# Hybrid streaming encoder: score products on all 128 rows, a plain first up unit, and convolution taps that alternate between channel halves

## The chip, the cores and the metric

The kernel runs on one core of one Trainium2 chip. The metric is the device time of one execution in microseconds (us). A core has a matrix engine (TensorE, PE in the profile, with PEld for its weight loads), a vector engine (VectorE, DVE), an activation engine (ScalarE, ACT), a general engine (GpSimd, POOL), and a sync engine (SyncE, SP) that here issues nearly all transfers. Each takes its own instructions in order and waits on semaphores for the others.

## What is computed

One layer of an encoder for 1024 prompt frames and 64 sample frames (T = 1088), model width 1024. A normed input goes through one projection into four mixers of width 256: a gated depthwise convolution of 31 taps, a "forgetting" attention (fox), a gated recurrence (hgrn), and a "stick-breaking" attention (sb). Then come an output projection, attention to 256 memory frames, and a feed-forward part. Cut to what matters:

```python
s = einsum('bqhd,bkhd->bhqk', q, k) * HEAD_DIM ** -0.5        # fox and sb: 4 heads of 64 each, 1024 x 1024, causal
fox: p = softmax(s + cq - ck);   sb: a = exp(log_sigmoid(z) + sum of log_sigmoid(-z) over later keys)
conv: y = depthwise_conv(a * sigmoid(g), 31 taps) + bias; layer norm over 256 channels; silu
x = x + mix @ w_out;  x = x + mem_attend(rmsnorm(x));  h = rmsnorm(x)
x = x + square(relu(h @ w_up)) @ w_down                       # 1024 -> 4096 -> 1024
```

The sample frames do the same with 512 cached keys ahead of their own.

## The kernel before

**Precision.** A product of two float32 operands is made of high and low parts (`split`, lines 168 to 171: ACT writes the high part, DVE the difference), and three matmuls: high by high, high by low, low by high (`mm3`). `mm` (line 71) issues every matmul.

**Order.** The kernel is written as lanes (projections, attention, convolution, recurrence), Python generators that a loop steps by a virtual clock. Each instruction gets a priority (`tc.cur_priority`, lower first), and a planner lays the instructions of each engine in one fixed order by priority and readiness. Projection matmuls have the lowest rank in the mixer stage (`PR_MM`), so they fill what the lanes leave of PE.

**Attention.** `project_qkv` makes queries, keys and values of a pair of heads (128 rows: head 0 on rows 0 to 63, head 1 on rows 64 to 127). Its sinks write `qT` (two buffers), `kT` (one) and `vn`, chunk by chunk (CH: 512, 256, 320 columns). There are four such pairs in turn: sb0, sb1, fox0, fox1, and `attend` (lines 527 to 597) runs for each. It splits the keys into `kh` and `kl`. For each block of 128 query rows (i = 0 to 7) with n = 128 (i + 1) keys it splits the query columns, makes the scores z of both heads, runs the softmax or stick-breaking chain on ACT and DVE, transposes the result (`key_T`) and multiplies by the values. A score product takes the 64 rows of its head, in three passes. Up to 512 keys both heads' products are issued together, pass by pass; over 512 keys there is one PSUM tile for both heads and they are made one after the other. After the eight blocks comes the sample block: a block-diagonal query tile `qbd` on 128 rows against 512 cached keys (`caches`) and 64 new ones.

**Convolution.** `lane_conv` takes three chunks (352, 352, and 320 prompt columns with 30 + 64 more, 414) and in each the two channel halves: load, gate, then 31 taps, the first a `tensor_scalar` and 30 `scalar_tensor_tensor` (line 773) that add into the same y.

**Feed-forward, up part.** Sixteen units of two column blocks of `w_up` each. A unit uses a Strassen-Winograd scheme: seven half products for eight, over sums of the four quarters of the normed activations (T1 to T4) and of the weights (S1 to S4). Group 0 of the columns (512) is normed early. Group 1 (576) is completed by `dense_add(1, w_mo, ...)`, which calls `forms(m)` after each of its eight row blocks: it adds to the sum of squares, and from m = 4 on it norms two blocks and builds B22, T1, T2, T3 and T4 on DVE and ACT. Everything after it is moved back by `tc.cur_priority += 1200`. Unit 0 then runs like the others, and computes the scale q of group 1 on its way. Unit 0 and unit 1 take B21 and B22 early. Weight tiles `wr`, `wh` and `wl` have two buffers each; the pool `ap` has 16.

Of the kernel before, what the change touches and what calls it, by code (L numbers as in the profile page):

```python
# [8 lines left out]
F32 = mybir.dt.float32  # L9
# [43 lines left out]
def kernel(ctx: ExitStack, tc: tile.TileContext, *args):  # L53
# [155 lines left out]
    hid_d = dram.tile([DFF // P, P, T], F32, name="hid_d")  # L209
    rms_d = dram.tile([P, 576], F32, name="rms_d")  # L210
# [31 lines left out]
    with ExitStack() as pa:  # L242
# [180 lines left out]
    def project_qkv(kind, hp, cq, ck, cv, cache_k, cache_v, outs):  # L423

        cs = slice(hp * P, (hp + 1) * P)
        qT = att.tile([P, T], F32, name="qT", tag="qT")
# [29 lines left out]
        tiles[kind, hp] = qT, kT, vn  # L456
# [70 lines left out]
    def attend(hp, kind, mask, chain, cache_k, cache_v, mix_slot):  # L527
        qT, kT, vn = tiles[kind, hp]
# [3 lines left out]
        hd = [slice(0, 64), slice(64, 128)]  # L532
        fox = kind == "fox"
        for i in range(8):
            n = P * (i + 1)

            zs, aTs = [None, None], []
            q = [wk.tile([P, P], F32R, name=nm, tag=nm, bufs=1) for nm in ("qh", "ql")]
            split(*q, qT[:, i * P:(i + 1) * P])

            def scores(heads):
                for h2 in heads:
                    zs[h2] = score_tile(n, h2)
                for c in range(0, n, 512):
                    w = min(512, n - c)
                    for t, (a, b) in enumerate(((0, 0), (1, 0), (0, 1))):
                        for h2 in heads:
                            mm(zs[h2][:, c:c + w], q[a][hd[h2]], k[b][hd[h2], c:c + w], t == 0,
                               t == 2 and c + w < n and not fox)
# [22 lines left out]
        n = PAST + SS  # L572

        for sl in hd:
            split(qbd[sl, 0, sl], qbd[sl, 1, sl], qT[sl, SP:T])
# [21 lines left out]
        yield 2  # L597
# [126 lines left out]
    CE = 320 + HW + SS  # L724

    def ct_(name, tag, n=CE):
        return hc.tile([P, n], F32, name=name, tag=tag)
# [14 lines left out]
    def lane_conv():  # L742
        tails = [None, None]
        for t0, np_ in ((0, 352), (352, 352), (704, 320)):
# [3 lines left out]
            for ct in range(2):  # L748
                yield Need(ct)
                yield Need(2 + ct)  # L750
                ext = ct_(f"ext{ct}", f"ce{ct}", CE + HW)
# [5 lines left out]
                if last:  # L757
                    V.tensor_copy(out=ext[:, HW + np_:CE - SS + HW], in_=hT[:, ct])
                    nc.sync.dma_start(out=ext[:, CE - SS + HW:], in_=pj_d[ct][:, SP:T])
# [4 lines left out]
                if last:  # L764
                    V.tensor_tensor(out=ext[:, CE - SS + HW:], in0=ext[:, CE - SS + HW:], in1=sg[:, np_:nt], op=ALU.mult)
# [3 lines left out]
                y = ct_(f"y{ct}", f"cy{ct}")  # L769
                V.tensor_scalar(out=y[:, :n], in0=ext[:, 0:n], scalar1=cwT[:, ct, 0:1], scalar2=cvec[:, 0, ct:ct + 1],  # L770
                                op0=ALU.mult, op1=ALU.add)
                for j in range(1, CW):
                    V.scalar_tensor_tensor(out=y[:, :n], in0=ext[:, j:j + n], scalar=cwT[:, ct, j:j + 1], in1=y[:, :n],  # L773
                                           op0=ALU.mult, op1=ALU.add)
                    if j % 3 == 2:
                        yield 0.15 + n / 300.0
                ys.append(y[:, :n])
                exts.append(ext)
            if last:
# [8 lines left out]
            sqs = [ct_(f"sq{ct}", f"ce{ct}", CE + HW) for ct in range(2)]  # L788
            for p0, pn in ((0, n // 2), (n // 2, n - n // 2)):
# [18 lines left out]
                for ct in range(2):  # L808
# [4 lines left out]
                    else:  # L813
                        nc.sync.dma_start(out=mix_d[ct][:, t0 + p0:SP], in_=ys[ct][:, p0:np_])
                        nc.sync.dma_start(out=mix_d[ct][:, SP:T], in_=ys[ct][:, CE - SS:])
# [207 lines left out]
    stage = [att.tile([P, 2 * n], F32, name="mix", tag=tag, bufs=b) for tag, b in (("qT", 2), ("kT", 1), ("vn", 2))]  # L1023
    stage = [t[:, i * n:(i + 1) * n] for t in stage for i in range(2)]
# [244 lines left out]
    for f in (T3, T4):  # L1269
        hb[f] = [[unit("xt" if k else "ap", F32R) for _ in range(2)] for k in range(4)]  # L1270

    sums2 = []

    def forms(m):
# [5 lines left out]
        if m < 4:  # L1280
            return
        k = m - 4
        (h11, h12), (h21, h22) = ((xw[0][i], xw[1][i]) for i in (k, k + 4))
        for i in (k, k + 4):
            normed(1, i, g_ffn, rm1, 0, N2, xw[1][i])
# [4 lines left out]
        split(*hb[B22][k], h22)  # L1290
# [36 lines left out]
    for i in range(NU):  # L1327
# [3 lines left out]
        split(*pa, r1)  # L1331
        s1 = fz.tile([P, 4, P], F32, name="s1", tag="s1", bufs=1)
# [11 lines left out]
        if i < 2:  # L1344
# [6 lines left out]
        plus(halves(c12), halves(c12 if i < 2 else t1), Z[:, :, :HN])  # L1351
        mul2(X, S1, hb[T1], True)
        plus(halves(c22), halves(t1), X[:, :, :HN])
        if i < 2:
# [5 lines left out]
        if i == 0:  # L1360
            q = rms_stats(1, psm, "w", s2=sums2[0])
            rms = unit("tm")
            nc.sync.dma_start(out=rms, in_=rms_d)
            V.tensor_tensor(out=q, in0=q, in1=rms, op=ALU.mult)
# [3 lines left out]
        if i >= 2:  # L1368
# [8 lines left out]
        for m, g, t in ((0, 0, c11), (0, 1, c12), (1, 0, c21), (1, 1, c22)):  # L1377
            t0, n, _ = GR[g]
            nc.sync.dma_start(out=hid_d[2 * i + m][:, t0:t0 + n], in_=t[:, :n])
# [125 lines left out]
```

## Time and profile before

| | us |
|---|---|
| median of 3 runs (1791.69 to 1795.78) | 1795.35 |
| the profiled execution, its own time | 1796.39 |
| its span, first to last instruction | 1794.7 |
| PE busy in the span | 1721.9 |
| DVE busy | 1179.9 |
| ACT busy | 793.2 |
| POOL busy | 103.2 |

The mean granted TensorE clock is 0.987 of full. A busy PE counts the pipeline's length of each matmul (some 0.28 us for a short one), so the step between starts, not the length, is what a matmul costs in a stream.

### The profile page before, as it was taken

What the parts mean: (1) busy time and instruction counts of PE and PEld (TensorE: products, weight loads), DVE (VectorE), ACT (ScalarE), POOL (GpSimd) and SP (SyncE); (2) the same over time, 40 slices, a digit from 0 to 9 for tenths busy, and PEclk for the clock granted to TensorE, in tenths of its full rate; (3) what the DMA queues carried; (4) which work ended last, traced back from release to release, by engine and by line L of the source; (5) the groups of instructions that cost most, each with busy time, mean ns of one, the idle gap of its engine ahead of it and who ended that gap; (6) DMA issues with size and microseconds to landing.
All of it is one profiled execution on the core that took longest, in us unless ns stands there. A gap on an engine that the chain in (4) does not pass through costs nothing.

```text
span 1794.7 us, 29493 instructions
## 1 busy us (share of the span) xinstructions
PE 1721.9 (96%) x11463; PEld 1511.7 (84%) x11475; DVE 1179.9 (66%) x2242; ACT 793.2 (44%) x1615; POOL 103.2 (6%) x201
## 2 busy tenths in 40 slices
PE   7999999999999999999999959999999999999997
PEld 5877757887877788988899949999999999999987
DVE  6455779888979886667777796555556544444435
ACT  6464566456356764346456343433344221222213
POOL 3011202000320210000000000000000000000000
PEclk9999999999999999999999989999999999999999
DMA  8221212222232448232522413333234823332112
GB/s 251 78 78 37 65 47 76 70 68 80 64 116 89 141 139 279 87 95 65 159 77 72 123 49 106 104 116 106 98 97 168 294 90 97 98 97 67 42 35 100
DMA packets 227307, 184.86 MB, mean 103 GB/s; under 512 B 16478, under 2 KB 196127, under 8 KB 227167
## 3 DMA queue, kind: packets, MB, share of 16 engines
q1 hardware_dynamic: 226911, 182.96, 32.7%
q8 instruction: 90, 1.47, 0.3%
q14 instruction: 50, 0.41, 0.1%
q0 software_dynamic: 256, 0.01, 0.0%
HBM read 132.45 MB, written 50.44 MB: 102 GB/s over the span
## 4 chain that ended last, share of the span: by engine, by line
PE 57%; DVE 5%; DMA 2%; ACT 1%; issue 1%; POOL 0%; SPq 0%; DVEq 0%; ACTq 0%; POOLq 0%
PE pz L71 23%; PE pw L71 16%; PE pa L71 8%; PE pq L71 5%; PE pmo L71 1%; PE pms L71 1%; DMA kr<-mkT_d 1%; PE pm L71 1%; DVE wl L171 1%; DVE ap L171 0%; PE pmt L1160 0%; PE pz L1430 0%; DVE tm L1075 0%; ACT wh L74 0%; DMA mix_d<-ho 0%
## 5 line engine op out<-in xcount | busy, mean ns | idle before, releaser
L74 ACT ACTIVATE wh<-wr 128x1024 fp32r<-128x1024 f32 (+1 forms) x180 | 161.4, 905 | 436.5 <-PE pz L71 196.3
L171 DVE TENSOR_TENSOR wl<-wr,wh 128x1024 fp32r<-128x1024 f32 (+1 forms) x180 | 184.6, 1032 | 70.8 <-ACT wh L74 69.8
L71 PE MATMUL pw<-ap,wh 128*128 128x512 f32 x704 | 219.7, 393 | 1.3 <-ACT t L74 0.7
L71 PE MATMUL pz<-ap,wh 128*128 128x288 f32 x960 | 192.5, 294 | 0.4 <-DVE ap L1325 0.4
L71 PE MATMUL pa<-ap,wh 128*128 128x256 f32 (+2 forms) x768 | 187.6, 332 | 2.6 <-DVE xt L1099 2.2
L71 PE MATMUL pm<-hx,wh 128*128 128x512 f32 (+1 forms) x640 | 176.3, 363 | 1.1 <-DVE hx L283 0.8
L71 PE MATMUL pm<-ap,wh 128*128 128x256 f32 (+1 forms) x768 | 164.2, 307 | 0.6 <-ACT vn L74 0.6
L71 PEld LDWEIGHTS pz<-ap,wh 128*128 128x128 f32 x960 | 156.7, 188 | 5.3 <-DVE ap L1325 0.8
L71 PEld LDWEIGHTS pw<-ap,wh 128*128 128x128 f32 x704 | 127.8, 189 | 23.7 <-ACT t L74 1.1
L71 PEld LDWEIGHTS pa<-ap,wh 128*128 128x128 f32 x768 | 132.9, 192 | 13.5 <-DVE xt L1099 2.4
L71 PE MATMUL pw<-ap,wl 128*128 128x512 f32 x352 | 138.1, 392 | 5.6 <-DVE wl L171 5.6
L71 PE MATMUL pz<-ap,wl 128*128 128x288 f32 x480 | 141.0, 294 | 0.0
L71 PEld LDWEIGHTS pm<-ap,wh 128*128 128x128 f32 x768 | 123.5, 191 | 5.4 <-issue 2.1
L71 PE MATMUL pa<-ap,wl 128*128 128x512 f32 (+2 forms) x384 | 127.2, 332 | 0.0
L71 PEld LDWEIGHTS pm<-hx,wh 128*128 128x128 f32 x640 | 110.2, 191 | 19.7 <-issue 1.9
L1325 DVE TENSOR_TENSOR xt<-xt,pz 128x576 f32<-128x576 f32 x56 | 42.2, 753 | 115.5 <-PE pz L71 111.0
L71 PE MATMUL pm<-ap,wl 128*128 128x256 f32 (+1 forms) x384 | 114.1, 297 | 0.0
L71 PE MATMUL pm<-hx,wl 128*128 128x512 f32 (+1 forms) x320 | 112.3, 351 | 0.0
L773 DVE SCALAR_TENSOR_TENSOR y<-ext,cwT,y 128x352 f32<-128x352 f32 (+1 forms) x180 | 106.4, 607 | 1.6
L1325 DVE TENSOR_TENSOR xt<-xt,pw 128x512 f32<-128x512 f32 (+2 forms) x80 | 51.0, 638 | 69.8 <-PE pw L71 67.7
L71 PE MATMUL pq<-ap,wh 128*128 128x512 f32 (+2 forms) x384 | 93.0, 331 | 0.0
L74 ACT ACTIVATE sba<-sba 128x127 f32<-128x127 f32 (+8 forms) x102 | 68.1, 682 | 52.8 <-DVE sba L490 52.0
(376 smaller groups left out, 3645.1 us busy)
## 6 DMA issues: line engine op xcount, KB each, us to landing
wr<-in_w_up_dram SPq DMA_DIRECT2D x32, 512.0 KB
wr<-in_w_down_dram SPq DMA_DIRECT2D x32, 512.0 KB
wr<-in_w_in_dram SPq DMA_DIRECT2D x24, 512.0 KB
hid_d<-ap SPq DMA_DIRECT2D x32, 288.0 KB
aq<-hid_d SPq DMA_DIRECT2D x32, 288.0 KB
wr<-in_w_out_dram SPq DMA_DIRECT2D x16, 512.0 KB
wr<-in_w_mq_dram SPq DMA_DIRECT2D x16, 512.0 KB
wr<-in_w_mo_dram SPq DMA_DIRECT2D x32, 256.0 KB
```

Of the source, the lines that this page charges most:

```text
L71: nc.tensor.matmul(out, lhsT=lhsT, rhs=rhs, start=start, stop=stop, **kw)
L74: nc.scalar.activation(out=out, in_=in_, func=func, **kw)
L171: V.tensor_tensor(out=lo, in0=src, in1=hi.bitcast(F32), op=ALU.subtract)
L773: V.scalar_tensor_tensor(out=y[:, :n], in0=ext[:, j:j + n], scalar=cwT[:, ct, j:j + 1], in1=y[:, :n], op0=ALU.mult, op1=ALU.add)
L1325: eng.tensor_tensor(out=out, in0=a, in1=b, op=ALU.add)
```

## The change

1. **Scores.** The query sink no longer fills `qT`: it writes a staging tile `st` and stores it to DRAM (`q_d`). `attend` loads it back as `q2`, each head's 64 rows twice, on rows 0 to 63 and 64 to 127 (four loads; one buffer). The keys are split as before, and three chained transfers per chunk swap halves so that `k[0]` holds head 0's high part over its low part and `k[1]` head 1's. A score product then runs on 128 rows in two passes (query high, query low), one head after the other; the low by low part comes along. The sample block moves ahead of the eight prompt blocks. The ninth tile of x at the start takes `kT`'s buffer instead of one of `qT`'s.
2. **Convolution.** Chunks of 376, 376 and 272 + 30 + 64 = 366 columns; the taps of the two halves alternate.
3. **First up unit.** Unit 0 uses plain products with the weights as they are (eight half products), of B11, B21, `b12` (new) and B22. After each row block of the last projection `second(m)` norms and splits that block only; `forms(k)` (T1 to T4) runs ahead of unit 1, with priority moved back by 800. The scale q is made between unit 0's two halves.

```diff
+    q_d = dram.tile([4, P, T], F32, name="q_d")
+    k_d = dram.tile([4, HD, SP], F32, name="k_d")
...
-            xt.append((att.tile([P, T], F32, name=f"xt{i}", tag=("vn", "qT")[i - 7])[:, :D] if i >= 7 else
+            xt.append((att.tile([P, T], F32, name=f"xt{i}", tag=("vn", "kT")[i - 7], bufs=(2, 1)[i - 7])[:, :D] if i >= 7 else
...
-        qT = att.tile([P, T], F32, name="qT", tag="qT")
+        slot = len(tiles)
...
-            V.scalar_tensor_tensor(out=qT[:, t0:t0 + n], in0=ps, scalar=HD ** -0.5, in1=rb[:, t0:t0 + n],
+            s = wk.tile([P, 512], F32, name="qT", tag="st")
+            V.scalar_tensor_tensor(out=s[:, :n], in0=ps, scalar=HD ** -0.5, in1=rb[:, t0:t0 + n],
                                    op0=ALU.mult, op1=ALU.mult)
+            nc.sync.dma_start(out=q_d[slot][:, t0:t0 + n], in_=s[:, :n])
...
+        q2 = att.tile([P, 2, T], F32, name="q2", tag="q2", bufs=1)
+        for h2 in range(2):
+            for sl in hd:
+                nc.sync.dma_start(out=q2[sl, h2], in_=q_d[slot][hd[h2]])
         k = [att.tile([P, T], F32R, name=nm, tag=nm, bufs=1) for nm in ("kh", "kl")]
         for t0, n in CH:
             split(*(t[:, t0:t0 + n] for t in k), kT[:, t0:t0 + n])
...
+            kh, kl = (t.bitcast(F32) for t in k)
+            nc.sync.dma_start(out=k_d[slot][:, cols], in_=kh[64:, cols])
+            nc.sync.dma_start(out=kh[64:, cols], in_=kl[:64, cols])
+            nc.sync.dma_start(out=kl[:64, cols], in_=k_d[slot][:, cols])
...
+            q = [wk.tile([P, 2, P], F32R, name=nm, tag=nm, bufs=1) for nm in ("qh", "ql")]
+            split(*q, q2[:, :, i * P:(i + 1) * P])
...
-                    for t, (a, b) in enumerate(((0, 0), (1, 0), (0, 1))):
-                        for h2 in heads:
-                            mm(zs[h2][:, c:c + w], q[a][hd[h2]], k[b][hd[h2], c:c + w], t == 0,
-                               t == 2 and c + w < n and not fox)
+                for h2 in heads:
+                    for c in range(0, n, 512):
+                        w = min(512, n - c)
+                        for t in range(2):
+                            mm(zs[h2][:, c:c + w], q[t][:, h2], k[h2][:, c:c + w], t == 0,
+                               t == 1 and c + w < n and not fox)
...
-        for t0, np_ in ((0, 352), (352, 352), (704, 320)):
+        for t0, np_ in ((0, CN), (CN, CN), (2 * CN, SP - 2 * CN)):
...
+            for j in range(CW):
+                for ct, (y, ext) in enumerate(zip(ys, exts)):
+                    if j == 0:
+                        V.tensor_scalar(out=y, in0=ext[:, 0:n], scalar1=cwT[:, ct, 0:1], scalar2=cvec[:, 0, ct:ct + 1],
+                                        op0=ALU.mult, op1=ALU.add)
+                    else:
+                        V.scalar_tensor_tensor(out=y, in0=ext[:, j:j + n], scalar=cwT[:, ct, j:j + 1], in1=y,
+                                               op0=ALU.mult, op1=ALU.add)
...
+    b12 = [pair(1) for k in range(4)]
...
-    def forms(m):
+    def second(m):
...
+        normed(1, m, g_ffn, rm1, 0, N2, xw[1][m])
+        split(*(hb[B22][m - 4] if m >= 4 else b12[m]), xw[1][m])
+
+    def forms(k):
...
-    dense_add(1, w_mo, HALF * P, KD - HALF, om[HALF:], ps1, store=True, after=forms)
+    dense_add(1, w_mo, HALF * P, KD - HALF, om[HALF:], ps1, store=True, after=second)
...
-    tc.cur_priority += 1200
...
+    ws = [load_w(w_up, 0, KD, m * P) for m in range(2)]
+    tiles = [unit("ap") for _ in range(4)]
+    for m in range(2):
+        W = bank()
+        mul(W, ws[m], hb[B11] + hb[B21], True, slice(0, N1))
+        square(tiles[2 * m][:, :N1], W)
+    q, rms = rms_stats(1, psm, "w", s2=sums2[0]), unit("tm")
+    nc.sync.dma_start(out=rms, in_=rms_d)
+    V.tensor_tensor(out=q, in0=q, in1=rms, op=ALU.mult)
+    for m in range(2):
+        Z = banks()
+        mul2(Z, ws[m], b12 + hb[B22], True)
+        square(halves(tiles[2 * m + 1]), Z[:, :, :HN], halves(q))
+    store_hidden(0, tiles)
+
+    for i in range(1, NU):
...
+        if i == 1:
+            tc.cur_priority += 800
+            for k in range(4):
+                forms(k)
```

## Rows read from the trace of the kernel before

**Rows 1.** Busy time of each engine by stretch (us from the span's start, length, then busy us and instructions of PE, PEld, DVE, ACT, POOL, the granted clock, the DMA share and GB/s).

```profile
60.00:200.00 140.00, 136.69 (x959) 111.39 (x958) 79.77 (x132) 78.09 (x155) 12.55 (x33) 0.98 0.22 63
200.00:500.00 300.00, 289.05 (x2095) 227.35 (x2098) 255.46 (x544) 164.62 (x371) 41.10 (x64) 0.99 0.23 67
500.00:650.00 150.00, 140.00 (x1124) 114.42 (x1130) 132.01 (x291) 98.62 (x240) 30.16 (x34) 1.00 0.38 114
1027.00:1077.00 50.00, 30.96 (x180) 26.40 (x179) 47.65 (x78) 24.07 (x42) 0.00 (x0) 0.83 0.24 71
```

**Rows 2.** PE's timeline from the end of the last projection into unit 0 (start us, us, engine, line, operation, tiles, shapes, count; in brackets the idle time before and what ended it).

```profile
1033.03 0.28 PE L71 MATMUL pa<-ap,wl 128*128 128x256 f32 x1
...
1045.29 1.44 PE L71 MATMUL pr<-tm,ones 128*128 128x320 f32 x2 [10.67 <-DVE tm L1054]
1052.36 0.80 PE L71 MATMUL pw<-ap,wl 128*128 128x512 f32 x1 [5.64 <-DVE wl L171]
...
1061.94 0.53 PE L71 MATMUL pz<-fz,wh 128*128 128x288 f32 x2 [0.34 <-ACT wh L74]
```

**Rows 3.** The chain that ended last, in order of time, over units 2 and 3 (start us, us, what, count).

```profile
1120.96 2.78 PE pw L71 x12
1123.73 6.36 PE pz L71 x48
1130.09 2.74 PE pw L71 x12
...
1142.10 2.78 PE pw L71 x12
```

**Rows 4.** The same chain at the end of the mixer stage, and below it the longest wait of the SP queue from 100 to 660 us (us in total, times, longest us).

```profile
612.28 2.32 DMA hq<-pj_d
...
665.30 4.53 DMA wr<-in_w_out_dram
...
672.21 7.80 PE pa L71 x26
...
SPq L416 <- DVE sp L415: 83.9, 19, 13.3
```

**Rows 5.** PE's timeline at a score block over 512 keys, behind four transposes (sb1, 768 keys).

```profile
266.62 0.60 PE L513 MATMUL pt<-ident,sba 128*128 128x128 f32 x4
267.15 0.50 PE L71 MATMUL z<-kh,qh 64*128 64x512 f32 x1
267.50 0.39 PE L71 MATMUL z<-kh,ql 64*128 64x512 f32 x1
267.73 0.39 PE L71 MATMUL z<-kl,qh 64*128 64x512 f32 x1
...
268.07 0.28 PE L71 MATMUL z<-kh,ql 64*128 64x256 f32 x1
268.19 0.28 PE L71 MATMUL z<-kl,qh 64*128 64x256 f32 x1
268.40 0.23 PE L71 MATMUL z<-mask_s,ident_bf 128*128 128x128 bf16 x1
```

**Rows 6.** PE's timeline at a score block of 128 keys (sb0, both heads in each row).

```profile
63.15 0.28 PE L71 MATMUL z<-kh,ql 64*128 64x128 f32 x2
63.27 0.28 PE L71 MATMUL z<-kl,qh 64*128 64x128 f32 x2
```

**Rows 7.** The view of tile z: one of its three groups of prompt score matmuls (count, ns min/median/max, first and last start, forms).

```profile
L71 PE MATMUL z<-kh,qh x96: 218/436/502, 63.0 to 610.1; 64*128 64x512 f32 x48, 64*128 64x128 f32 x16, 64*128 64x256 f32 x16, 64*128 64x384 f32 x16
```

**Rows 8.** DVE's timeline: three taps of one half in a row, and six that take the halves in turn.

```profile
418.43 1.83 DVE L773 SCALAR_TENSOR_TENSOR y<-ext,cwT,y 128x352 f32<-128x352 f32 x3
...
426.70 3.06 DVE L773 SCALAR_TENSOR_TENSOR y<-ext,cwT,y 128x352 f32<-128x352 f32 x6
```

**Rows 9.** Views of the tiles qT, kT and mix_d (low parts on DVE, and the stores of the four sample blocks); then timelines: the first scores of sb1 on PE, the store of fox0's sample block on SP, the first and third query chunk of fox1 on DVE.

```profile
L171 DVE TENSOR_TENSOR ql<-qT,qh x32: 268/284/537, 62.7 to 600.3; 128x128 fp32r<-128x128 f32 x32
...
L171 DVE TENSOR_TENSOR kl<-kT,kh x12: 419/484/692, 36.7 to 513.1; 128x512 fp32r<-128x512 f32 x4, 128x256 fp32r<-128x256 f32 x4, 128x320 fp32r<-128x320 f32 x4
...
L596 SPq DMA_DIRECT2D mix_d<-os x4: 320/326/338, 197.3 to 643.5; - x4
...
212.60 0.33 PE L71 MATMUL z<-kh,qh 64*128 64x128 f32 x2
...
480.94 0.32 SPq L596 DMA_DIRECT2D mix_d<-os  x1
...
535.76 0.67 DVE L432 SCALAR_TENSOR_TENSOR qT<-pm,rb 128x512 f32<-128x512 f32 x1
...
553.57 0.49 DVE L432 SCALAR_TENSOR_TENSOR qT<-pm,rb 128x320 f32<-128x320 f32 x1
```

**Rows 10.** Timelines at the start: the first write of kT on DVE and the last transposes of x on PE.

```profile
34.46 0.68 DVE L437 TENSOR_TENSOR kT<-pm,rb 128x512 f32<-128x512 f32 x1
...
41.32 0.58 PE L280 MATMUL px<-ident,xt 128*128 128x128 f32 x3
```

**Rows 11.** Busy time by stretch, as in the first group, for the gap ahead of the units.

```profile
1034.00:1064.00 30.00, 11.92 (x43) 8.17 (x44) 29.43 (x46) 15.37 (x27) 0.00 (x0) 0.72 0.04 13
```

**Rows 12.** Groups of DVE instructions from 1034 to 1064 us by shape (count | busy us, mean ns | idle before).

```profile
L171 DVE TENSOR_TENSOR fz<-xt,fz 128x576 fp32r<-128x576 f32 x5 | 3.8, 751 | 0.0
...
L171 DVE TENSOR_TENSOR wl<-wr,wh 128x1024 fp32r<-128x1024 f32 x1 | 1.2, 1218 | 0.0
```

More of the change, by code (lines that the diff above doesn't have):

```diff
@@ L455, in project_qkv @@
         flush()
-        tiles[kind, hp] = qT, kT, vn
+        tiles[kind, hp] = slot, kT, vn
         done.add((kind, hp))
@@ L572, in attend @@
+            n = min(n, SP - t0)
+            cols = slice(t0, t0 + n)
+            kh, kl = (t.bitcast(F32) for t in k)
+            nc.sync.dma_start(out=k_d[slot][:, cols], in_=kh[64:, cols])
+            nc.sync.dma_start(out=kh[64:, cols], in_=kl[:64, cols])
+            nc.sync.dma_start(out=kl[:64, cols], in_=k_d[slot][:, cols])
         n = PAST + SS
-        for sl in hd:
-            split(qbd[sl, 0, sl], qbd[sl, 1, sl], qT[sl, SP:T])
+        for h2, sl in enumerate(hd):
+            split(qbd[sl, 0, sl], qbd[sl, 1, sl], q2[sl, h2, SP:T])
@@ L597, in attend, with scores @@
         yield 2
+        for i in range(8):
+            n = P * (i + 1)
+            zs, aTs = [None, None], []
+            q = [wk.tile([P, 2, P], F32R, name=nm, tag=nm, bufs=1) for nm in ("qh", "ql")]
+            split(*q, q2[:, :, i * P:(i + 1) * P])
+            def scores(heads):
+                for h2 in heads:
+                    zs[h2] = score_tile(n, h2)
+                for h2 in heads:
+                    for c in range(0, n, 512):
[3 more added lines that the diff above has]
+                               t == 1 and c + w < n and not fox)
+                for h2 in heads:
+                    if fox:
+                        for c in range(0, n, 512):
+                            w = min(512, n - c)
+                            mm(zs[h2][:, c:c + w], neg1[:, 2 * hp + h2], ckx[:, c:c + w], False, c + w < n)
+                    mm(zs[h2][:, n - P:n], ident_bf, mask[0], False, True)
+            if n <= 512:
+                scores((0, 1))
+            for h2 in range(2):
+                if n > 512:
+                    scores((h2,))
+                p = chain(zs[h2][:, :n], n)
+                aTs.append(key_T(p, n))
+                yield 0.3 + n / 256.0
+            pv = ps_tr.tile([P, P], F32, name="pv", tag="tr")
+            for j in range(i + 1):
+                for h2 in range(2):
+                    mm(pv[hd[h2]], vn[:, j, hd[h2]], aTs[h2][:, j], j == 0, j == i)
+            o = wk.tile([P, P], F32, name="o", tag="o")
+            evac(o, pv)
+            nc.sync.dma_start(out=mix_d[mix_slot][:, i * P:(i + 1) * P], in_=o)
     prev = [None]
@@ L768, in lane_conv @@
                     V.tensor_copy(out=tails[ct], in_=ext[:, n:n + HW])
[L769 to L777, printed above, removed]
-                exts.append(ext)
+                ys.append(ct_(f"y{ct}", f"cy{ct}")[:, :n])
+                exts.append(ext)
+            for j in range(CW):
[6 more added lines that the diff above has]
+                                               op0=ALU.mult, op1=ALU.add)
+                if j % 3 == 2:
+                    yield 0.3 + n / 150.0
             if last:
@@ L787, in lane_conv @@
             rs = ct_("rs", "c0").rearrange("p (j n) -> p j n", j=2)
-            sqs = [ct_(f"sq{ct}", f"ce{ct}", CE + HW) for ct in range(2)]
+            sqs = [ct_(f"sq{ct}", f"ce{ct}", CN + HW) for ct in range(2)]
             for p0, pn in ((0, n // 2), (n // 2, n - n // 2)):
@@ L1022 @@
     n = GR[0][1]
-    stage = [att.tile([P, 2 * n], F32, name="mix", tag=tag, bufs=b) for tag, b in (("qT", 2), ("kT", 1), ("vn", 2))]
-    stage = [t[:, i * n:(i + 1) * n] for t in stage for i in range(2)]
+    stage = [att.tile([P, 2 * n], F32, name="mix", tag=tag, bufs=b) for tag, b in (("kT", 1), ("vn", 2))]
+    stage.append(att.tile([P, 4 * n], F32, name="mix", tag="q2", bufs=1))
+    stage = [t[:, i * n:(i + 1) * n] for t in stage for i in range(t.shape[1] // n)]
     stage += [wk.tile([P, n], F32, name="mix", tag="st") for _ in range(2)]
@@ L1295, in forms @@
         split(hb[T4][k][0][:, :N1], hb[T4][k][1][:, :N1], h21[:, :N1])
-    dense_add(1, w_mo, HALF * P, KD - HALF, om[HALF:], ps1, store=True, after=forms)
+    dense_add(1, w_mo, HALF * P, KD - HALF, om[HALF:], ps1, store=True, after=second)
     pm1.close()
     psm = ctx.enter_context(tc.tile_pool(name="psm", bufs=2, space=PSUM))
-    tc.cur_priority += 1200
+    for f in (T3, T4):
+        hb[f] = [[unit("xt" if k else "ap", F32R) for _ in range(2)] for k in range(4)]
     for t in t1s:
@@ L1325, in plus, with store_hidden @@
         eng.tensor_tensor(out=out, in0=a, in1=b, op=ALU.add)
-    for i in range(NU):
+    def store_hidden(i, tiles):
+        for m, g, t in zip((0, 0, 1, 1), (0, 1, 0, 1), tiles):
+            t0, n, _ = GR[g]
+            nc.sync.dma_start(out=hid_d[2 * i + m][:, t0:t0 + n], in_=t[:, :n])
+    ws = [load_w(w_up, 0, KD, m * P) for m in range(2)]
[13 more added lines that the diff above has]
+    for i in range(1, NU):
         r1 = fetch_w(w_up, 0, KD, 2 * i * P)
@@ L1359 @@
         square(c11[:, :N1], W)
[L1360 to L1364, printed above, removed]
         mul2(Z, S3, hb[T3], False)
@@ L1367 @@
         square(c22, c22, q)
-        if i >= 2:
+        if i > 1:
             mul2(X, S4, hb[B22], False)
@@ L1376 @@
         square(c21[:, :N1], c21[:, :N1])
-        for m, g, t in ((0, 0, c11), (0, 1, c12), (1, 0, c21), (1, 1, c22)):
-            t0, n, _ = GR[g]
-            nc.sync.dma_start(out=hid_d[2 * i + m][:, t0:t0 + n], in_=t[:, :n])
+        store_hidden(i, (c11, c12, c21, c22))
     fz_ctx.close()
```

66 lines of the change are left out of this document (14 added, 52 removed).

## The prediction

> **What bounds the kernel now.** First the busy times by stage [rows 1]. From 60 to 650 us, the mixer stage, TensorE (PE) is busy 566 of 590 us, VectorE (DVE) 85% from 200 to 500 and 88% from 500 to 650. From 1027 to 1077 us it is the reverse: PE 30.96 of 50 us, DVE 47.65. So two places are on the path that sets the end: a PE-bound mixer stage with DVE close behind, and a gap at the head of the feed-forward stage where PE waits for DVE. I read the gap in PE's timeline [rows 2]: the last matmul of the projection before it starts at 1033.03, then PE idles 10.67 and 5.64 us behind DVE, and full-rate products begin at 1061.94. Behind it the chain of waits is PE alone, in steady units: from one unit's first pw at 1120.96 to the next at 1142.10 is 21.1 us [rows 3], so unit 2 began at 1120.96 - 21.1 = 1099.8. The mixer's end is mixed: the chain passes a load of the gated recurrence's last chunk at 612.28, then PE and the others in turn, then a weight load at 665.30, and the output projection starts at 672.21 [rows 4].
>
> **The scores on PE.** A pass of 512 keys takes 267.73 - 267.50 = 0.23 us, 256 keys 0.12 (268.19 - 268.07) [rows 5]; 384 I put between, at 0.17. Rows of up to 512 keys (i = 0 to 3): both heads' matmuls of 128 keys are one merged row of 0.28, and the next pass of both starts 63.27 - 63.15 = 0.12 later [rows 6], so the heads run side by side and three passes cost three steps. After the change they need four: 0.12 + 0.12 + 0.17 + 0.23 = 0.64 us more for each of four attends, +2.6. Rows over 512 keys (i = 4 to 7) run one head at a time; a pass over them is 4 x 0.23 + 0.64 = 1.56 us, and one of three goes for 2 heads x 4 attends: -12.5. Passes alone: -10.
> The other part is the tile form. The transposes ahead of a score block run on 128 x 128; four of them from 266.62 to 267.15 take 0.53 where 4 x 0.11 = 0.44 is their step; the first score matmul takes 267.50 - 267.15 = 0.35 instead of 0.23; the last takes 268.40 - 268.19 = 0.21 instead of 0.12 [rows 5]. That is 0.09 + 0.12 + 0.09 = 0.30 us a block. The code has 48 blocks; PE's order breaks them into 84 unbroken runs between the first (63.0) and the last (610.1) of the 96 matmuls of kh with qh [rows 7]. The new score matmuls use 128 rows like their neighbours, so 84 x 0.30 = 25 us goes (48 blocks: 14; none, if the 0.30 is a wait for operands: 0). I take 25, since blocks of every attend show it: PE is freed 35 us (10 to 35).
> The Trainium skill, TensorEngine Tiling (Array Packing), section Key Properties, says that changing the tiling mode drains the engine, and that separate tiles work in parallel. The second speaks against the change: were it so in all rows, three side-by-side passes would become four everywhere and PE would lose some 9 us by this step, an estimate. The rows show both: side by side up to 512 keys, one head after the other above.
>
> **How much of the 35 is kept.** From 60 to 200 DVE is 57% busy and a fourth of it, 9 us, should be kept whole. From 200 to 650 DVE has 387.5 us of work [rows 1]. The taps change it: three in a row of one half take 1.83, 0.61 each, and six that alternate halves 3.06, 0.51 each [rows 8]; 64 of the 180 taps follow their own half, counted in DVE's timeline, so 64 x 0.1 = 6.4 us goes (the rest, the third chunk above all, alternates already; 376 columns for 352, and 366 for 414, leave the sum at 1118). The doubled query split adds DVE 0.42 - 0.28 = 0.14 x 32 = 4.3 us [rows 9]. Left: 385.4. If DVE can be packed to the 88% it reaches from 500 to 650, that takes 385.4/0.88 = 438 us, 12 less than 450. Kept: 9 + 12 = 21 (none to 35).
>
> **New transfers and waits.** Queries go to DRAM after each projected chunk and come back doubled; the load waits for the third chunk. In the last attend the first chunk is written at 535.76, the third at 553.57 [rows 9]. A DRAM load of 192 KB shows 2.32 us on the chain, one of 512 KB 4.53 [rows 4]; a store and then four loads of 272 KB that share the queues I bound by 2 x 2.3 and 2.3 + 2 x 4.5, 5 and 11 us, and take 8. So an attend's prompt rows start 18 + 8 = 26 us later than now. The three chained key moves per chunk hold SP's queue twice each, some 2.3 us per wait; behind it wait weight loads and spills (SP waits up to 13.3 us there already [rows 4]), and weights are fetched a projection ahead. The sample block, moved from the end of the attend to its head with its two cache loads, two qbd splits and its store, covers the key moves. I cost these at nothing for PE: projections fill its queue, and the attention lane's last store, at 643.5 [rows 9], comes 28 us before 672.21; if that cover is gone, it is the slower rival.
> At the start x's ninth tile now holds kT's only buffer. Its last transposes end at 41.9, kT's first write is at 34.46 [rows 10]: PE could lose 0 to 7.5 us, and can bring those transposes forward meanwhile; I take 2, near the lower end. Mixer: 21 - 2 = 19 us saved.
>
> **The first up unit.** Units 0 and 1 now take from 1033.3 to 1099.8: 66.5 us. Plain unit 0 has 2 x (24 pw + 48 pz): 12 pw are 2.75, 48 pz 6.36 [rows 3], so 2 x (5.5 + 6.36) = 23.7, 2.6 above the fast form; unit 1 21.1; the sums of squares 1: 45.8. That leaves 20.7 us of wait, and the lower clock in it (granted 0.72 of full from 1034 to 1064, so partly 1.2 GHz [rows 11]).
> What is late next: the combined forms, now built under unit 0. DVE is full (29.43 of 30 [rows 11]) until 1063.3. New ahead of unit 1's first form product: four lo parts of 0.67 (each group of 576 takes 0.75, its successor starts 0.08 before its end [rows 12]), two weight splits of 1.14 by the same overlap; the scale chain, five operations over 576 columns in two pieces, 4.3, and two squares of 0.75, which today come after: 10.8, to 1074; 3.1 of it (last T3, T4, S3, A22) is not needed yet: 1071. PE needs them after 23.7 + 2.75 + 2.75 + 3.2 from 1033.3: 1065.7. Stall 5 (0, if DVE's order is better, to 15, if buffers of ap and wh free late). Saved 20.7 - 5 = 16 us.
> SP's moved DMAs there (hidden stores, the rms_d load) only wait shorter. The down stage is untouched: 0.
>
> **Sum.** Profiled execution: span 1794.7, time 1796.4, 1.0 above the median 1795.35 of the three. 1796.4 - 19 - 16 = 1761.4; less 1.0: 1760.
>
> **Rivals.**
> A, DVE and the lanes bind: DVE stays at the present 86%, 385.4/0.861 = 448, 2 us less, and the first attend keeps only part of its 9: mixer 5 instead of 19. For it: DVE's 85 to 88% beside serial lanes; against: PE's 96%. 1796.4 - 5 - 16 - 1 = 1774.
> B, the 0.30 is no cost of form but a wait that stays: freed 10, kept 10 - 2 = 8: 1771. Against it: four transposes in a row step evenly until the score block follows.
> C, the stall moves to unit 1 (15 us): only 6 saved there: 1770. For it: eight of sixteen ap buffers hold b12 until unit 0 ends, and unit 1's forms need six.
> D, all is kept, 35 + 20.7, and the start costs nothing: 1740.
> E, slower: the attention lane becomes the bound. The four attends end with their sample stores (the first at 197.3, the third at 480.94, the last at 643.5) and begin with a first score or query chunk (the second at 212.60, the fourth at 535.76) [rows 9]: gaps of 15, 55 and, behind the last, 28 us, and the one I leave unread taken as 15, 113 in all. A delay of 26 each, 104, just fits; it decides from 28. If q2 or key moves sit once per attend behind an SP wait like the 13.3, the delay is 39, 157 in all, 44 over: 1795 + 44 - 16 = 1823. Against it: in today's rows the short query rows of the first 18 us run at PE's and DVE's leisure, and would be quicker later.
>
> **Chances.** Forecast 0.50 (own range 1750 to 1769); A 0.20, a fifth of it within 0.3% of no change; B 0.06; C 0.08; D 0.08; E 0.08. A measurement here tells apart about 0.3%, 5 us. Faster 0.88, same 0.04, slower 0.08. The range leaves out E, half of D and the end of A: 1744 to 1782.
>
> **What the profile after would show.** Score matmuls on 128*128 with steps of 0.23 and no 0.35 at a block's head; 192 prompt score matmuls for 288; mixer end near 653; taps never 0.61 apart; the first hidden product right behind the last pa, with no idle over 2 us, and one stall of some 5 us in unit 1; clock full from there on. Wrong would be: PE idle over 30 us in the mixer (A or E: ended by DVE and ACT in A, by q2's or the keys' DMA in E), a first score block still at 0.35 (B), a gap over 10 us in unit 1 (C).

## The result, and the profile after

The changed kernel takes 1773.51 us (median of 4 runs, 1772.48 to 1775.03) where the kernel before, beside it, took 1794.06 (1791.69 to 1795.78): a ratio of 0.9876 [0.9853, 0.9899], 22 us by the ratio and 24.1 by the two profiled spans (1794.7 and 1770.6). The forecast was 1760, a gain of 35; the range to 1782 holds it. A third of the gain is missing. Three marks on PE show where: the first and the last `pa` matmul before the feed-forward stage, and the end. Before they are at 672.21 [rows 4], 1033.03 [rows 2] and 1794.7.

| stretch, us | before | after | won | forecast |
|---|---|---|---|---|
| start to first pa | 672.2 | 645.9 | 26.3 | 19 |
| first pa to last pa | 360.8 | 374.3 | -13.5 | 0 |
| last pa to the end | 761.7 | 750.4 | 11.2 | 16 |

So the mixer stage won more than was forecast, and the stage behind it, for which the forecast had nothing, lost half of it again. First the windows of the changed kernel (columns as in [rows 1]).

```profile
60.00:200.00 140.00, 136.28 (x962) 115.77 (x961) 86.24 (x141) 78.60 (x157) 14.66 (x32) 1.00 0.33 93
200.00:500.00 300.00, 288.04 (x2180) 234.30 (x2179) 260.80 (x550) 171.05 (x380) 36.94 (x66) 1.00 0.31 87
500.00:645.00 145.00, 134.47 (x1105) 113.15 (x1104) 119.14 (x266) 100.75 (x249) 22.41 (x34) 0.96 0.47 137
645.00:675.00 30.00, 20.25 (x94) 16.04 (x91) 27.58 (x60) 12.11 (x28) 0.00 (x0) 0.77 0.70 233
...
1020.00:1046.00 26.00, 25.36 (x153) 22.94 (x152) 25.93 (x42) 15.54 (x26) 0.00 (x0) 1.00 0.30 96
1046.00:1060.00 14.00, 7.48 (x30) 5.45 (x29) 13.96 (x23) 8.85 (x16) 0.00 (x0) 0.83 0.10 40
```

The fourth row is the seam between mixer and output projection: PE is busy 20 of 30 us, DVE 28, and the granted clock is 0.77. With two levels, full and half, that is 30 x 0.23 / 0.5 = 14 us at half. The next two fences show what PE waits for: its timeline there, and the chain that ended last (start us, us, what).

```profile
645.33 0.61 PE L71 MATMUL pv<-aT,vn 128*64 128x128 f32 x8
645.86 1.20 PE L71 MATMUL pa<-ap,wh 128*128 128x512 f32 x4
655.68 0.61 PE L802 MATMUL pco<-ident,ext 128*30 128x128 f32 x2 [8.62 <-DVE cvo L804]
657.42 0.80 PE L71 MATMUL pa<-ap,wl 128*128 128x512 f32 x1 [1.12 <-DVE wl L171]
```

```profile
644.09 10.28 DVE y L794 x21
...
655.32 0.31 DVE cvo L804
655.63 0.60 DVE ap L171
656.23 1.15 DVE wl L171
...
657.42 3.36 PE pa L71 x7
```

DVE's order holds the last 22 conv taps (`y`) in a row, behind them the copy `cvo` that frees the conv lane's one PSUM buffer for PE's `pco`, and only then the low parts (`ap`, `wl`) of the output projection. PE makes the four products that need high parts alone and stands still for 8.6 us. The view of tile ext says when the taps end, in the changed kernel and, below it, in the kernel before:

```profile
L794 DVE SCALAR_TENSOR_TENSOR y<-ext,cwT,y x180: 582/602/1358, 286.9 to 654.7; 128x376 f32<-128x376 f32 x120, 128x366 f32<-128x366 f32 x60
...
L773 DVE SCALAR_TENSOR_TENSOR y<-ext,cwT,y x180: 559/585/1307, 300.5 to 641.9; 128x352 f32<-128x352 f32 x120, 128x414 f32<-128x414 f32 x60
```

In the kernel before the last tap started at 641.9, 30 us ahead of the first pa; here at 654.7, 9 us behind it. Now the scores: a block over 512 keys on PE (768 keys of sb1, as in [rows 5]) and a group of the view of tile z, to be held against [rows 7].

```profile
293.39 0.66 PE L517 MATMUL pt<-ident,sba 128*128 128x128 f32 x4 [0.50 <-ACT sba L74]
293.81 0.48 PE L71 MATMUL z<-kh,qh 128*128 128x512 f32 x1
294.13 0.39 PE L71 MATMUL z<-kh,ql 128*128 128x512 f32 x1
294.36 0.28 PE L71 MATMUL z<-kh,qh 128*128 128x256 f32 x1
294.47 0.28 PE L71 MATMUL z<-kh,ql 128*128 128x256 f32 x1
294.60 0.23 PE L71 MATMUL z<-mask_s,ident_bf 128*128 128x128 bf16 x1
```

```profile
L71 PE MATMUL z<-kh,qh x48: 225/409/502, 90.3 to 622.1; 128*128 128x512 f32 x24, 128*128 128x128 f32 x8, 128*128 128x256 f32 x8, 128*128 128x384 f32 x8
```

Four such groups make 192 products for 288, all on 128 rows. The transposes hand over after 0.42 us (0.53 before), the last product after 0.13 (0.21), but the first product of 512 keys still takes 0.32, not 0.23. At the start (DVE, then PE; compare [rows 10]) kT's first write comes 9.7 us later, and PE idles ahead of it:

```profile
44.13 0.68 DVE L441 TENSOR_TENSOR kT<-pm,rb 128x512 f32<-128x512 f32 x1
```

```profile
40.86 1.46 PE L282 MATMUL px<-ident,xt 128*128 128x128 f32 x6 [0.94 <-ACT xs L74]
43.71 1.41 PE L71 MATMUL pr<-dg,ones 128*128 128x128 f32 x4 [1.40 <-DVE dg L272]
```

Last the up units on PE, where [rows 2] had gaps of 10.67 and 5.64 us, and two rows of the chain for the steady units [rows 3].

```profile
1021.08 0.69 PE L71 MATMUL pw<-ap,wh 128*128 128x512 f32 x2 [0.64 <-DVE xt L1119]
...
1045.92 0.62 PE L71 MATMUL pw<-ap,wh 128*128 128x512 f32 x2
...
1049.51 0.73 PE L71 MATMUL pw<-ap,wh 128*128 128x512 f32 x2 [0.69 <-ACT t L74]
...
1058.31 0.85 PE L71 MATMUL pz<-fz,wh 128*128 128x288 f32 x2 [5.78 <-ACT wh L74]
...
1060.58 0.68 PE L71 MATMUL pz<-fz,wh 128*128 128x288 f32 x2
...
1061.30 0.68 PE L71 MATMUL pz<-fz,wh 128*128 128x288 f32 x2
...
1062.49 0.43 PE L71 MATMUL pz<-fz,wh 128*128 128x288 f32 x2
...
1062.89 0.43 PE L71 MATMUL pz<-fz,wh 128*128 128x288 f32 x2
```

```profile
1097.33 2.78 PE pw L71 x12
...
1118.47 2.78 PE pw L71 x12
```

Unit 0 follows the last pa at once. The wait has gone into unit 1, 0.69 + 5.78 us, while DVE is full (13.96 of 14 us), and behind it a round of three products takes 0.72 us (1060.58 to 1061.30) instead of 0.40 (1062.49 to 1062.89).

### The profile page after: what moved, and what is told of

Its sections match the earlier page's. It is cut to its first block, busy times and chain, and to the rows that moved or that the text cites. A ratio compares the mean times of both kernels' runs of the same rounds, so it can differ in the third digit from the quotient of the medians.

```text
span 1770.6 us, 29390 instructions
## 1 busy us (share of the span) xinstructions
PE 1698.2 (96%) x11379; PEld 1506.6 (85%) x11379; DVE 1174.6 (66%) x2231; ACT 791.5 (45%) x1614; POOL 93.6 (5%) x201
## 4 chain that ended last, share of the span: by engine, by line
PE 78%; DVE 13%; ACT 4%; DMA 2%; issue 2%; POOL 0%; SPq 0%; DVEq 0%; POOLq 0%; ACTq 0%
PE pz L71 25%; PE pw L71 16%; PE pm L71 11%; PE pa L71 9%; PE pq L71 5%; PE z L71 2%; DVE y L794 2%; PE pmo L71 2%; PE pms L71 1%; PE po L71 1%; PE pt L517 1%; PE pv L71 1%; DVE hsc L933 1%; DVE sba L494 1%; DVE wl L171 1%
## 5 line engine op out<-in xcount | busy, mean ns | idle before, releaser
L71 PE MATMUL pw<-ap,wh 128*128 128x512 f32 x720 | 223.4, 391 | 1.3 <-ACT t L74 0.7
L71 PE MATMUL pz<-ap,wh 128*128 128x288 f32 x988 | 198.3, 294 | 0.0
L71 PEld LDWEIGHTS pz<-ap,wh 128*128 128x128 f32 x988 | 161.3, 188 | 4.7
L71 PEld LDWEIGHTS pw<-ap,wh 128*128 128x128 f32 x720 | 130.1, 188 | 24.1 <-ACT t L74 1.1
L71 PE MATMUL pz<-ap,wl 128*128 128x288 f32 x494 | 145.5, 294 | 0.0
L794 DVE SCALAR_TENSOR_TENSOR y<-ext,cwT,y 128x376 f32<-128x376 f32 (+1 forms) x180 | 101.1, 609 | 0.3
L71 PEld LDWEIGHTS pz<-ap,wl 128*128 128x128 f32 x494 | 92.7, 188 | 0.0
```

The source lines that it names most:

```text
L71: nc.tensor.matmul(out, lhsT=lhsT, rhs=rhs, start=start, stop=stop, **kw)
L794: V.scalar_tensor_tensor(out=y, in0=ext[:, j:j + n], scalar=cwT[:, ct, j:j + 1], in1=y, op0=ALU.mult, op1=ALU.add)
```

## The experiments

**Theory 1**: PE's shorter mixer leaves DVE less time; the conv lane, last in rank on DVE, collects what is missing, and its taps land ahead of the low parts that the output projection needs. **Theory 2**: the conv edit itself makes the conv lane late. A rival within theory 1: DVE has no time for these taps anywhere, so that no order helps. All ratios are to the kernel before on the same chip.

**The first up unit alone** (the kernel before with the diff's hunks from `forms` on, and none ahead of them).

> The kernel before with the plain first up unit alone; scores, keys, queries and conv as before. The changed kernel won 11.3 us from its last pa on, where 16 were forecast. If that stage stands for itself: 11 us faster than before, some 1783, with a wait of 5 to 6 us in unit 1 and the clock at half there. If the stage starts in another state when the mixer is unchanged (other clock, other order of DVE): the forecast 16, some 1778. The windows up to 1020 us should not move by more than 1 us.

1784.06 us, 0.9943 [0.9927, 0.9958], 10 us faster. The wait is nearly the same (6.38 us in unit 1, for 5.78): the part stands for itself, and 16 was too much. The windows did move, by 2.5 us at the first pa, more than I had allowed.

**The conv edit alone** (the kernel before with the diff's hunks in `ct_` and `lane_conv`).

> The kernel before with the conv edit alone: chunks of 376, 376 and 272 (366 with the two histories) for 352, 352 and 320 (414), taps of the halves in turn. Theory 1 (PE's shorter mixer leaves DVE less time, and the conv lane, last in rank, collects what is missing): alone the edit takes work off DVE and PE sets the pace, so 0 to 4 us faster than before, 1790 to 1794, and no wait at the first w_out products. Theory 2 (the edit itself puts the conv lane late, since both halves must be there before the first tap): 5 to 10 us slower, 1799 to 1804, with the last chunk's taps between PE's last mixer product and the first low parts of the output projection, as in the changed kernel.

1795.5 us, 1.0003 [0.9993, 1.0013]: nothing won, nothing lost. Theory 2 falls as the cause of the loss: the last tap starts at 651.2, 9 us later than before, but still 18 us ahead of the first pa. Of the 39 us by which this margin shrinks in the changed kernel (from 30 ahead to 9 behind), 26 are the earlier first pa.

**The changed kernel with the taps of a half in a row** (chunk sizes as changed, the loop over the taps inside the loop over the halves as before).

```
-            for j in range(CW):
-                for ct, (y, ext) in enumerate(zip(ys, exts)):
+                for j in range(1, CW):
+                    V.scalar_tensor_tensor(out=y[:, :n], in0=ext[:, j:j + n], ...)
```

> The changed kernel with the taps of one half in a row, as before; the new chunk sizes stay. Theory 1: DVE has about 6 us more to do in a stage where it has none to spare, so the seam at the output projection grows by up to that: 1774 to 1780. Theory 2: the conv lane is no longer late, the 8.6 us wait and the half clock at the seam go: 1760 to 1764.

1775.06 us, 0.9891 [0.9878, 0.9904]; the interval overlaps the changed kernel's, so the tap order is worth little here, and not the cause.

**Scores and chunk sizes alone** (the diff's hunks up to `attend`, the one on `stage`, and `CN` and `CE` in `lane_conv`; taps and FFN of before).

> The kernel before with the scores on 128 rows and the conv chunk sizes of the changed kernel (without them the tiles do not fit the memory), taps in the order of before, FFN of before. Theory 1: this is the changed kernel's mixer with 6 us more of DVE work: the same wait of 8 us or more at the first w_out products, and 7 to 13 us faster than before, 1781 to 1787. Theory 2: without the new tap order the mixer's whole gain of 26 us stays: 1768 to 1771. If freed PE time is small without the taps (the 28 us came from elsewhere), PE's sum of steps up to the first w_out product stays above 625.

1786.1 us, 0.9955 [0.9943, 0.9967], 8 us. The first pa comes 24 us earlier (647.8), the last pa only 13 (1020.2): so the loss at the seam is there without the new tap order and the plain unit. Since the conv edit by itself, chunk sizes included, shows no loss, it comes with the scores. This and the up unit, 8 + 10, make up 18 of the 22.

**Which of PE's steps were the tile form's.** The same products on rows 0 to 63 alone; this leaves out what the keys' low parts add.

```
-  mm(zs[h2][:, c:c + w], q[t][:, h2], k[h2][:, c:c + w], t == 0,
+  mm(zs[h2][:, c:c + w], q[t][:64, h2], k[h2][:64, c:c + w], t == 0,
```

> The changed kernel with its two score passes over rows 0 to 63 alone: same passes, same columns, same order, but tiles of 64 x 128 between neighbours of 128 x 128; it leaves out the products of queries with the keys' low parts. Tile form theory (0.30 us at each of some 84 blocks): PE's sum of steps up to the first w_out product grows by 20 to 25 us, the first pa comes at 660 to 671, and 1784 to 1798 in all. Rival B (the 0.30 was a wait that has nothing to do with the tile's rows): no change on PE, 1772 to 1775.

1779.19 us, 0.9922 [0.9908, 0.9936], between the two expectations: 5.7 us slower than the changed kernel by the medians. The same block on PE:

```profile
298.74 0.65 PE L517 MATMUL pt<-ident,sba 128*128 128x128 f32 x4
299.32 0.50 PE L71 MATMUL z<-kh,qh 64*128 64x512 f32 x1
299.66 0.39 PE L71 MATMUL z<-kh,ql 64*128 64x512 f32 x1
...
300.01 0.27 PE L71 MATMUL z<-kh,ql 64*128 64x256 f32 x1
300.22 0.23 PE L71 MATMUL z<-mask_s,ident_bf 128*128 128x128 bf16 x1
```

On 64 rows the way in takes 0.58 for 0.42 and the way out 0.21 for 0.13, but the first product 0.34 for 0.32. So 0.24 of this block's cost is the form's, and the long first product is not: it is there on 128 rows too (the middle of 21 such steps behind transposes is 0.32 on 128 rows and 0.34 on 64). PE's steps from 62 us to the first pa, each to the next start (or to its own end, if PE then idles), summed over the trace's records:

```
us                      before   after   rows 0 to 63 alone
all steps                583.1   557.5   569.4
scores, masks included    81.2    63.2    70.1
transposes of key_T       43.6    33.2    40.3
idle                      27.1    26.2    19.3
```

Form: 70.1 - 63.2 + 40.3 - 33.2 = 14.0 us, or 0.175 for each of the 80 unbroken runs that these two kernels have (the kernel before has 84). From the kernel before to this run: 81.2 - 70.1 = 11.1 in the scores, which is the pass saved, and 43.6 - 40.3 = 3.3 in the transposes, which a pass does not touch; order and clock differ there too (seven of the transposes before run at half clock), and no run takes this part by itself. Rival B, in which none of it is form, falls. And of the 11.9 us that the whole sum differs here, 6.9 are idle again in the changed kernel: at that point DVE and the lanes do hold the mixer, but only by half.

**The seam: rank of the last conv chunk.** Its columns, from 752 on, are needed only by the projection's second group. The loop over the two cache rows (`pco`, `cvo`) moves up from behind the taps, and the taps get a later rank.

```
+            if last:
+                for at, dst in ((np_, conv_p), (CE, conv_s)):
...
+                tc.cur_priority = PR_END + 150
             for j in range(CW):
...
-            if last:
-                for at, dst in ((np_, conv_p), (CE, conv_s)):
...
```

> The changed kernel with the last conv chunk's taps ranked behind the first work of the output projection (its columns, 752 and up, are needed only by the projection's second group), and the two conv cache rows taken out ahead of its taps. Theory 1, order: the projection waits only because DVE's fixed order has 22 taps ahead of the low parts; then the idle 8.6 us and the 13.7 us at half clock (worth up to 6.8) go: 1758 to 1765. Rival, throughput: DVE has not the time for this work anywhere before the second group, so the wait comes back there or at its first rms: 1769 to 1774, or slower.

1765.34 us, 0.9844 [0.9829, 0.9859], 8 us faster than the changed kernel by the medians, 5.7 by the ratios. The window at the seam:

```profile
645.00:675.00 30.00, 28.17 (x126) 22.87 (x125) 27.37 (x45) 9.74 (x13) 0.00 (x0) 1.00 0.87 279
```

DVE does as much as without the mend (27.4 us, 27.6), in another order; PE is busy 28 of the 30 us and the granted clock is full. First to last pa takes 363.1 us for 374.3.

**Either half of that mend by itself**, since the edit had two. First without the rank, against the kernel just shown:

```
-                tc.cur_priority = PR_END + 150
```

> The changed kernel with only one half of the mend at the seam: the two conv cache rows (pco, cvo) taken out ahead of the last chunk's taps, the taps' rank as it was. If PE waits there for the cache rows' copy, which stands behind the taps and holds the one PSUM buffer: the wait goes, 1764 to 1767, as with both halves (1765). If it waits for the low parts behind the same taps: the wait stays and only changes its name, 1771 to 1775.

1773.18 us, 0.9882 [0.9862, 0.9902], no gain. The wait only changed its name, as PE's timeline shows:

```profile
645.25 1.20 PE L71 MATMUL pa<-ap,wh 128*128 128x512 f32 x4
655.59 1.59 PE L71 MATMUL pme<-y,ones 128*128 128x183 f32 x4 [9.15 <-DVE y L802]
657.84 0.79 PE L71 MATMUL pa<-ap,wl 128*128 128x512 f32 x1 [0.66 <-DVE wl L171]
```

Then the rank alone, the cache rows staying behind the taps:

```
+            if last:
+                tc.cur_priority = PR_END + 150
             for j in range(CW):
```

> The changed kernel with only the other half: the last chunk's taps ranked behind the first work of the output projection, the cache rows still taken out behind them. If the rank is what counts: 1764 to 1767. If the cache rows on PE's fixed order then hold the projection until the taps are done: 1772 or more.

1771.37 us, 0.9872 [0.985, 0.9894], and neither of the two that I expected. The seam is clean (PE 29.76 of 30 us from 645 to 675), but the conv lane, its cache rows now behind all taps, ends at 700.0 instead of 693.7, and a wait turns up at the second group, which needs its columns:

```profile
705.69 1.21 PE L71 MATMUL pa<-ap,wh 128*128 128x320 f32 x4 [2.41 <-ACT ap L74]
...
728.76 0.80 PE L71 MATMUL pa<-ap,wh 128*128 128x256 f32 x2 [2.79 <-DVE xt L1121]
```

The first of these waits, 2.41 us, is new. The second, 2.79, is only longer: the changed kernel waits 2.16 us there and the kernel before 2.15. In all, PE idles 9.7 us from first to last pa, for 3.8 with both halves and 13.4 in the changed kernel. So the rival of theory 1 is right to this extent: there is a second due time, and moving the work only helps if it meets that one too.

**The same rank without the scores** (conv edit, rank and moved cache rows in the kernel before).

> The kernel before with the conv edit and the last conv chunk ranked behind the first work of the output projection; scores and FFN of before. If the conv lane's lateness at the seam comes only with PE's shorter mixer (theory 1), there is little to win here: first to last pa takes 363 us without this rank, 360.8 in the kernel before: 1791 to 1795. If the rank is worth its 8 us in any of these kernels, 1786 to 1788, and the wait at the seam had nothing to do with the scores.

1798.6 us, 1.0013 [1.0, 1.0026]: nothing to win, and 3.6 us above the range that I gave for that. So the late conv lane comes with the scores edit, as theory 1 has it. That it comes by PE's shorter mixer, and not by another part of that edit (the doubled split on DVE, the transfers, the moved sample block), is argued and not shown. In the run on rows 0 to 63 the first pa comes 4.9 us later (650.7), and the last tap too (659.6), with the same 18 taps behind the first pa. So between these two kernels the lag does not change with PE's time in the run: it stands in DVE's fixed order.

**The start.**

```
-  tag=("vn", "kT")[i - 7], bufs=(2, 1)[i - 7]
+  tag=("vn", "q2")[i - 7], bufs=(2, 1)[i - 7]
```

> The changed kernel with x's ninth tile in the buffer of the doubled queries (not needed before the first attend) in place of kT's. The prediction priced the shared buffer at 2 us. If so: 1771 to 1772. If the start costs what the trace shows (the first query chunk 68.5 for 61.7, a clock dip of 6.8 us at 41.6): 5 to 7 us, 1767 to 1769. If DVE and the conv lane, not PE's start, set the mixer's end: 1773 to 1774, with the seam's wait grown by what PE wins.

1768.63 us, 0.9859 [0.9844, 0.9874]: 3.0 us by the ratios, 4.9 by the medians. kT's first write is back at 37.18, and PE is busy 47.10 us to 60 (45.03 in the changed kernel, first row; 47.73 before). The shared buffer cost 3 to 5 us, not 2.

```profile
0.00:60.00 60.00, 45.03 (x240) 36.30 (x241) 34.37 (x86) 31.74 (x67) 19.30 (x67) 0.94 0.73 219
...
0.00:60.00 60.00, 47.10 (x257) 38.22 (x258) 35.50 (x88) 32.07 (x68) 20.40 (x67) 0.97 0.75 224
```

**Two plain units**, the combined forms built under both.

```
+    for u in range(2):                  # the plain unit, for u = 0 and 1
...
-    for i in range(1, NU):
+    for i in range(2, NU):
```

> The changed kernel with units 0 and 1 plain and the combined forms built under both. If unit 1's wait of 5.8 us, and the 6.8 us at half clock behind it, come from DVE having 20 us too little time for the forms: the wait goes, 5.8 + 3.4 saved, and a plain unit costs 23.7 - 21.1 = 2.6: 1766 to 1768. If the wait is one for buffers (eight of sixteen ap hold the plain operands): it moves to unit 2 and the 2.6 is added: 1774 to 1777.

1765.65 us, 0.9847 [0.9833, 0.986], 8 us faster than the changed kernel by the medians, 5.2 by the ratios. From the last pa to unit 2 PE has no wait left, and DVE has 10 us to spare:

```profile
1019.00:1069.00 50.00, 49.37 (x301) 45.08 (x300) 39.38 (x61) 23.65 (x39) 0.00 (x0) 1.00 0.29 95
```

Unit 1's wait was DVE's time, not a buffer.

**All three mends together.**

> The changed kernel with all three edits that won time by themselves: last conv chunk behind the first work of the output projection, x's ninth tile in the buffer of the doubled queries, units 0 and 1 plain. Alone, each against the changed kernel by their ratios to the kernel before: 0.9844, 0.9859 and 0.9847 beside 0.9876, so 5.7, 3.0 and 5.2 us, and by the medians 8, 5 and 8. If they are three places that stand for themselves, the sum: 1753 to 1760. If the mixer's end is set by DVE once the start and the seam are mended, the start's part is lost: 1757 to 1763.

1753.95 us (1752.51 to 1754.6), 0.9761 [0.9744, 0.9779]: the three add up (8, 5 and 8 us by the medians), and this version is 20 us faster than the changed kernel and 41 faster than the one before. Seam, output projection, and the first two units:

```profile
642.00:672.00 30.00, 29.94 (x133) 24.70 (x134) 27.25 (x46) 9.70 (x14) 0.00 (x0) 1.00 0.90 291
672.00:1006.00 334.00, 329.07 (x2066) 299.49 (x2065) 241.51 (x523) 169.36 (x365) 0.24 (x2) 0.99 0.34 103
1006.00:1056.00 50.00, 49.37 (x299) 45.02 (x299) 39.16 (x62) 23.92 (x39) 0.00 (x0) 1.00 0.29 94
```

## Why the prediction was right, and where it was wrong

The measured 1773.5 lies in the range of 1744 to 1782, but outside the 1750 to 1769 that the prediction gave its own mechanism. That the range held is in part luck: of the three stretches in the first table the first won 7 us more than forecast, and this hides half of what the second lost.

**The scores on PE.** Ten for the pass and 25 for the form were forecast; 11.1 (and 3.3 in the transposes) and 14.0 were measured, 28.4 of 35. The form's 0.30 us a block was mis-sized: 0.12 of it, the long first product, was read off a row as a cost of the form because the next product is shorter, and it is no such thing. The remaining 0.18 x 84 would have been 15.

The Trainium skill, TensorEngine Tiling (Array Packing), section Key Properties, says that a change of the tiling mode drains TensorE. The traces agree in that the change of form costs time, 14.0 us over these blocks; the drain itself is not seen in them.

**How much is kept: the step that failed.** The prediction kept 21 of 35, by packing all of DVE's mixer work ahead of the mixer's end. PE kept nearly all: its idle time to the first pa hardly moved (27.1 and 26.2). DVE was not packed tighter: from 200 to 645 us it is busy 379.9 of 445 us, 85%, not 88. But its work did not have to fit, since the planner let the lane of lowest rank slide: 18 conv taps begin behind the first pa, none before. Then the debt fell due in the stage behind, for which the prediction's sum has no term: 13.5 us there. Net, 12.8 us instead of 19. Windows from the first to the last pa, each with its stretches at half clock below it, show what the 13.5 are made of (the changed kernel, then the kernel before):

```profile
645.86:1020.44 374.58, 361.14 (x2204) 325.26 (x2202) 270.97 (x567) 180.89 (x383) 0.24 (x2) 0.98 0.38 116
649.10:662.80 13.70, 5.99 (x16) 4.64 (x17) 12.30 (x24) 1.07 (x3) 0.00 (x0) 0.50 0.67 218
...
672.21:1033.31 361.10, 357.70 (x2184) 323.34 (x2184) 251.09 (x520) 175.12 (x362) 0.24 (x2) 0.99 0.39 120
673.40:676.80 3.40, 3.40 (x9) 2.64 (x9) 2.29 (x5) 1.91 (x4) 0.00 (x0) 0.50 0.83 250
738.30:741.70 3.40, 3.40 (x19) 3.40 (x18) 2.36 (x4) 0.68 (x1) 0.00 (x0) 0.50 0.16 35
```

PE idles 13.4 us for 3.4, which is 10.0 of the 13.5, above all the waits of 8.6 and 1.1. Of the rest, 3.1 are the conv lane's own products (`pme`, `pva`, `pco`), which now stand behind the first pa. The half clock explains next to nothing: PE is busy in 6.0 of its 13.7 us, and the kernel before has 6.8 us at half clock in this stage with PE busy throughout; the steps of all `pa` products add up to 195.4 us for 195.0. The rank and cache row edits win back 11.2 of the 13.5 in the profiled stretch, so this was the order of DVE's work more than its amount. Rival A gave 1774, the measured time, and its condition held (DVE at 85%). But its mechanism, DVE holding the mixer's end, shows only in part (the 6.9 us of new idle above); what tells them apart is the place of the wait.

**Transfers and the attention lane.** Costed at nothing, and PE shows no wait for q2's or the keys' DMA in the rows above. The delay itself was read rightly: the first score product starts at 90.3 for 63.0 (views of tile z), 27 us later where 26 were forecast. But the cover is used up: the 28 us between the lane's end and the first pa are now none, since PE's last `pv` (645.33) runs straight into the first pa. Rival E did not come, though the next cut in PE's time may well meet that lane.

**The start.** 2 us taken from a bound of 0 to 7.5; 3 to 5 measured. The prediction saw PE's idle time there but not that its clock would drop as well (0.94 to 60 us, 1.00 before and 0.97 with the other buffer).

**The taps.** 6.4 us of DVE's time were counted as a gain; the taps' steps add up to 100.4 us before, 98.0 with the conv edit alone and 97.3 in the changed kernel, so it was 2.4 to 3.1. Alone the edit gave nothing (1.0003). In the changed kernel its worth, 1773.5 against 1775.1, is inside the intervals.

**The first up unit.** 16 forecast, 11.2 measured. From the last pa to unit 2 (1097.33 less one unit of 21.14, so 1076.2) it takes 55.8 us from 1020.4, where 50.8 was forecast. Of the 5.0 more, 0.8 is unit 0 (25.5 for 24.7), 1.5 the wait (6.5 for 5), and 2.7 unit 1's own products, of which those up to 1062 run at half clock. The wait's place, size and cause were right, and that the forms are late next; that the clock falls behind a wait was not in the sum. Rival C needed over 10 us there and a shortage of buffers; two plain units rule that out. Of the list of signs, 192 products, the first hidden product right behind the last pa and the stall of 5 us came; the mixer's end near 653, the full clock, and a head of a score block without the long step did not.

What stays open: by which part of the scores edit the conv lane falls behind in DVE's order, and the 3.3 us in the transposes.

## What to carry to other kernels

When PE gets shorter beside a full second engine, look up which lane has the lowest rank there, when its work is really due, and what stands behind it in that engine's fixed order: the gain is kept at the first mark and can be lost at the next. Rank work by its due time (the last chunk's columns were needed some 58 us after the first pa, 703.3 and 644.9 in the run with the rank alone), and check the next due time as well, since half a mend only moved the wait. And before pricing a step as a cost of some form, find the same step in a neighbour without that form.

## What the runs showed of the hardware

The first product of 512 columns of a score block takes 0.32 us to the next start on 128 rows and 0.34 on 64, where the second takes 0.23: it comes with the head of a block, not with the tile's rows, and why is not shown. Entering and leaving 64-row products between 128-row neighbours cost 0.16 + 0.08 us at the block shown and 0.175 on average (14.0 us over 80 runs). After a wait of 6 to 9 us the products ran at half clock for a while, so that the rounds of three products took 0.72 us for 0.40; the kernel with all three mends, which has no such wait, shows 1.00 in the same stretches. Shorter waits had it behind them too: in the kernel before, a wait of 2.15 us ends at 737.58, and 3.4 us at half clock follow from 738.3.
